# Half of an expert table and its sub-keys laid out by feature ahead of the launch, and a quarter of a dot fewer per block

## The chip, the cores and the metric

The kernel runs on one core of a Trainium2 chip. A core has TensorE (PE in the profile; its weight loads are PEld), VectorE (DVE), ScalarE (ACT), GpSimd (POOL) and SyncE (SP); sixteen DMA engines move data between the memory outside (HBM) and the core's SBUF. TensorE writes its results to PSUM, eight banks of 128 x 512 float32. SP issues plain loads and stores, POOL the indirect loads that gather rows by a list of indices. Each engine runs its own instructions in their order and waits on semaphores for the others.

The metric is the device time of one execution in microseconds (us), the median of several runs. The work that the host does to lay arrays out ahead of the launch is not in it.

## The reference, cut to what matters

One layer of a decoder over 256 prompt tokens and 8 x 4 sample tokens: a projection, two groups of heads (RWKV-7 and sparse attention), an output projection with a layer norm, and then the part that the change touches, a mixture of 16384 experts, each one row of two tables `u_tab` and `v_tab` (16384 x 2048, float32):

```python
def peer_ffn(x, wq, subkeys, u_tab, v_tab):
    q = (xt @ wq).reshape(n, P_HEADS, 2, P_DKEY // 2)
    s = jnp.einsum('nhcd,hckd->nhck', q, subkeys).astype(jnp.float32)
    hv, hix = lax.top_k(s, P_TOPK)
    ...
    tv, tpos = lax.top_k(cand, P_TOPK)
    expert = jnp.take_along_axis(cand_e, tpos, axis=-1)
    gate = jax.nn.softmax(tv, axis=-1).astype(x.dtype)
    ...
        h = jax.nn.gelu(jnp.einsum('cd,chkd->chk', xb, u_tab[eb]), approximate=False)
        return jnp.einsum('chk,chkd->cd', gb * h, v_tab[eb])
```

Eight heads choose 16 experts for each token, by scores against 2 x 8 sets of 128 sub-keys. For each choice the token's vector is multiplied with a row of `u_tab`.

## The kernel before

The kernel is one function, `hybrid_decode_step`, in stages; `kernel` around it hands the arrays over and starts it. Its pools of tiles lie on the left and the right of SBUF, and a tile that takes the place of an older one waits until that is free. The order of the instructions on each engine is made when the program is built: a scheduler simulates a timeline and takes what it holds to be ready, unless `high_priority`, `issue_after` or `keep_in_program_order` say otherwise. A load that moves to another place in that simulated time thus shifts its neighbours too.

The stages that matter here:

- **Sample rows** (`sample_chain`, up to some 1124 us). The 32 sample tokens run through output projection, queries, scores and their own dots, with weights loaded into a ring of ten buffers (`cw`). `subkeys` (L1424) loads the sub-keys as 128 rows of 128, turns them with 16 transposes on TensorE and copies them from PSUM into SKT on ScalarE (L1432). The last step is a Gelu on ScalarE (L1560) behind the last dot.
- **`wq`** (to some 1240 us). A second SKT is made in the same way for the prompt tokens. Then 16 chunks of `peer_wq` are multiplied with the tokens laid out by feature, XT, in float32 (L1813), the result is copied into QP (L1814), scored against SKT (L1370), and VectorE finds the top 16.
- **`peer`**, the dense loop, `for i1 in range(P): dense(i1)`. The product of the tokens with `u_tab` is split by features. The second half, features 1024 to 2047, is computed densely: for all 16384 experts, in 128 blocks of 128. A block's table rows are loaded by SP into `ur` (L1844, 128 x 1024, three buffers, NUR), turned by eight transposes on TensorE into PSUM `pt` (L1849), and split into two float32r parts: `uh`, rounded by ScalarE (L1644), and `ul`, the remainder, by VectorE (L1645). The tokens have been split in the same way into XHd and XLd. Three products of the parts, for eight blocks of 128 features, make 24 matmuls (L1855) into `ph`, which ScalarE copies to AW (L1857).
- **Dots.** The first half, features 0 to 1023, is done only for the chosen experts: POOL gathers 128 table rows of 1024 (L449, tile `rows`, five buffers, NRW), one for each token of a tile, and VectorE multiplies them with the tokens and sums along the row (L1779). There are 256 of these dots. Five or six are done in `wq`; the loop does ND = 1 per block and one more in NDN of 8 blocks; the rest, `left`, is spread over the first 28 steps of the next stage.
- **`weigh`**. 64 steps pick each choice's value out of AW: VectorE makes one-hot rows (L1887, `oo`), TensorE multiplies (L1899, L1929), VectorE sums (L1910, `xj`). The order here is held as written.
- **V**. The second table's half of the work, a dense product with `v_tab`. The change does not touch it.

Of the kernel before, what the change touches and what calls it, by code (L numbers as in the profile page):

```python
# [11 lines left out]
F32R = mybir.dt.float32r  # L12
# [6 lines left out]
P = 128  # L19
# [3 lines left out]
NPR = 256  # L23
# [12 lines left out]
WB = 4  # L36
# [10 lines left out]
NDW = 1  # L47
NPRI = 12
ND = 1
NDN = 4  # L50
NUR = 3
NRW = 5
WF = 3
PRO = 400
PRR = 0
# [90 lines left out]
def hybrid_decode_step(ctx: ExitStack, tc: tile.TileContext, a, outs, dbg=None):  # L146
    nc = tc.nc
    ve, sc, pe, gp, sy = nc.vector, nc.scalar, nc.tensor, nc.gpsimd, nc.sync
    stop = dbg.get("stop", 99) if dbg is not None else 99
# [99 lines left out]
    ident = C0("ident")  # L249
# [1131 lines left out]
    def choose(t, h, pool, S, TV):  # L1381
# [39 lines left out]
        ve.reciprocal(sm8, sm8)  # L1421
        ve.tensor_tensor(ge, ge, sm8[:, :, None].to_broadcast([P, n, 16]), OP.mult)

    def subkeys(raw, dst, tag):  # L1424

        for hf in range(2):
            sy.dma_start(raw[hf], a["peer_subkeys"][0].rearrange("h c k d -> k (h c) d")[:, 8 * hf:8 * hf + 8])
        for q in range(4):
            pb = bank(tag)
            for e in range(4):  # L1430
                pe.transpose(pb[:, 128 * e:128 * e + 128], raw[q // 2][:, 4 * (q % 2) + e, :], ident)
            sc.copy(dst[:, 4 * q:4 * q + 4, :].rearrange("p a b -> p (a b)"), pb)  # L1432

    def gate_rows(t_, u_):

        sy.dma_start(t_, a["rwkv_g2"][0, 0:128, :])
# [26 lines left out]
    utab, vtab = a["peer_u"][0], a["peer_v"][0]  # L1463
# [6 lines left out]
    def sample_chain(cx):  # L1470
        ring = lambda: cx([P, 1024], "cw", bufs=NCW)
        g2a, g2b = ring(), ring()
        gate_rows(g2a, g2b)
        pb = bank("ss")
# [56 lines left out]
        turned(X1s, x1s)  # L1531
        yield 1
        SKT, QPs, TV = cx([P, 16, P], "SKT"), cx([P, 16, 32], "QPs"), cx([P, 2, 16], "TV2")
        subkeys([ring().rearrange("p (k d) -> p k d", k=8) for _ in range(2)], SKT, "ss")
        yield 1
        qs = cx([P, 512], "qs", tag="xr_")

# [85 lines left out]
    def x1c(t, c0, n):  # L1623

        return X1[t][c0 // 1024][:, c0 % 1024:c0 % 1024 + n]
# [16 lines left out]
    def columns(pb, xh, xl):  # L1642

        sc.copy(xh, pb)  # L1644
        return ve.tensor_tensor(xl, pb, xh.bitcast(F32), OP.subtract)  # L1645
# [67 lines left out]
    bp_.close()  # L1713
    xq = Pool("xq", "right")
    XT = xq([P, 16, NPR], "XT")
    XH, XL = (xq([P, 8, NPR], nm, F32R) for nm in ("XHq", "XLq"))

    M_("ln1")
    gb1 = {}
# [4 lines left out]
    for t in range(2):  # L1724
        layer_norm(lp, lambda c0, n: x1c(t, c0, n),
                   *(lambda c0, n, nm=nm: gb1[nm, c0 // 1024][:, c0 % 1024:c0 % 1024 + n] for nm in ("ln1_g", "ln1_b")))
        for hf in range(2):
            sy.dma_start(X1D[P * t:P * t + P, 1024 * hf:1024 * hf + 1024], X1[t][hf])
        for q in range(4):
            pb = bank("pa")  # L1730
            for e in range(4):
                pe.transpose(pb[:, 128 * e:128 * e + 128], x1c(t, 512 * q + 128 * e, 128), ident)
            tk = slice(P * t, P * t + P)
            k4, p4 = slice(4 * (q % 2), 4 * (q % 2) + 4), pb.rearrange("p (k t) -> p k t", k=4)
            sc.copy(XT[:, 4 * q:4 * q + 4, tk], p4)
            if q > 1:
                columns(p4, XH[:, k4, tk], XL[:, k4, tk])
    oe.close()
    lp.close()
    cx[0].close()  # L1740
# [14 lines left out]
    HD = [up([P, P], f"hd{t}") for t in range(2)]  # L1755
    TV = [up([P, 8, 16], f"TV{t}") for t in range(2)]
    kc, dp, kq = (Pool(nm, "left") for nm in ("kc", "dp", "kq"))
    XHd, XLd = dp([P, 8, NPR], "XHd", F32R), dp([P, 8, NPR], "XLd", F32R)
    SKT = kq([P, 16, P], "SKT")
    QP = kq([P, 16, NPR], "QP")  # L1760

# [37 lines left out]


    kw_ = Pool("kw", "right")
    subkeys([kw_([P, 8, P], "wraw", bufs=WB) for _ in range(2)], SKT, "pb")
    hits = []
    for h in range(9):
        S = []
        for c in (2 * h, 2 * h + 1):
            if c < 16:
                pb = bank("pj")
                for o in range(0, 16, 8):
                    w = kw_([P, 8, P], "wraw", bufs=WB)  # L1810
# [18 lines left out]
    kw_.close()  # L1829
    sc.copy(XHd, XH)  # L1830
    sc.copy(XLd, XL)
    xq.close()
    kq.close()
    M_("peer")
    banks(pt=3, ph=2, pb=3)
    for t in range(2):
        gates(t, up, TV[t])
    aw = Pool("aw", "right")
# [1 line left out]

    def dense(i1):

        w = dp([P, 1024], "ur", bufs=NUR)
        sy.dma_start(w, utab[P * i1:P * i1 + P, 1024:])  # L1844
        ph = bank("ph")
        for q in range(2):
            pb = bank("pt")
            for e in range(4):
                pe.transpose(pb[:, 128 * e:128 * e + 128], w[:, 512 * q + 128 * e:512 * q + 128 * e + 128], ident)  # L1849
            wh, wl = dp([P, 4, P], "uh", F32R, bufs=2), dp([P, 4, P], "ul", F32R, bufs=2)  # L1850
            with tc.high_priority(offset=120 + 45 * i1 if i1 < NPRI else 0):
                lo_ = columns(pb.rearrange("p (k t) -> p k t", k=4), wh, wl)
            for e in range(4):
                for wi, xi in ((wh, XHd), (wh, XLd), (wl, XHd)):
                    mm = pe.matmul(ph[:, :NPR], wi[:, e, :], xi[:, 4 * q + e, :NPR],  # L1855
                                   start=(q == 0 and e == 0 and wi is wh and xi is XHd), stop=(q == 1 and e == 3 and wi is wl))
        return lo_, mm, sc.copy(AW[:, i1 // 64, :, i1 % 64], ph[:, :NPR])  # L1857

    tabled = []
    for i1 in range(P):  # L1860
        lo_, mm, end = dense(i1)
        n_ = ND + (i1 * NDN % 8 < NDN)
        with tc.issue_after(lo_.ins):
# [86 lines left out]
    raw = {}  # L1950
# [29 lines left out]
    pb = bank("pb")  # L1980
# [50 lines left out]
    for k in range(P):  # L2031
# [90 lines left out]
```

## Time and profile before

| | us |
|---|---|
| three runs | 2581.37, 2557.7, 2567.01 |
| median | 2567.01 |
| the profiled execution, its own time | 2586.08 |
| its span, first to last instruction | 2583.8 |
| mean granted TensorE clock | 0.93 |

The page begins with the busy time of each engine over the whole span:

```profile
PE 2310.9 (89%) x17452; PEld 1961.9 (76%) x17452; DVE 1939.6 (75%) x4264; ACT 1014.9 (39%) x1852; POOL 1328.2 (51%) x1393
```

Then it cuts the span into 40 slices of 64.6 us; each digit is the busy share in tenths, PEclk the granted clock:

```profile
PE   7989999988889987389799999996699799989996
DVE  4789756553654549859987888889976689888988
PEclk9999999987888978689899999996899899999998
DMA  7877974456579848975599999996678689898894
```

The dense loop is the run of slices with 9 in PE and DMA at once (some 1240 to 1740 us, slices 20 to 27). Two of the costliest groups of the page, by line (operation, output from inputs, shapes, count; busy us and mean ns of one; idle time of the engine just before them, and what ended it):

```profile
L449 POOL DMA_INDIRECT rows<-in_peer_u,gi x256 | 302.6, 1182 | 308.5 <-DVE rows L1779 273.9
L1849 PE MATMUL pt<-CT,ur 128*128 128x128 f32 x1024 | 149.4, 274 | 0.0
```

The mean of one matmul is its latency; since matmuls are pipelined, the time between two starts is shorter and is read from the chain or the timeline. A dot is an instruction L1779 with a short one that reads its sum; here too the next begins before the last one's recorded end.

### The profile page before, as it was taken

The numbers are of one execution on the slowest core, as the hardware profiler recorded it, in microseconds if no ns is written. First come the engines' busy times: TensorE is split into PE (matmuls) and PEld (weight loads), VectorE is DVE, ScalarE is ACT, GpSimd is POOL, SyncE is SP. The second block draws the span as 40 slices with busy tenths as digits, with TensorE's granted clock in tenths as the row PEclk, the third lists the DMA queues.
The fourth block names the chain that finished last, engine by engine and source line by source line (L and its number), as shares of the span: only waits on it lengthen the run. The fifth ranks groups of instructions, "written<-read, shape, count | busy, mean of one in ns | idle before, by whom it ended". The sixth has DMA issues, their size and how long they took to land.

```text
span 2583.8 us, 47156 instructions
## 1 busy us (share of the span) xinstructions
PE 2310.9 (89%) x17452; PEld 1961.9 (76%) x17452; DVE 1939.6 (75%) x4264; ACT 1014.9 (39%) x1852; POOL 1328.2 (51%) x1393
## 2 busy tenths in 40 slices
PE   7989999988889987389799999996699799989996
PEld 7878898866455655268799999996576688878885
DVE  4789756553654549859987888889976689888988
ACT  3433222223433432211244444444466444444443
POOL 6677424232543107636544444445555577767772
PEclk9999999987888978689899999996899899999998
DMA  7877974456579848975599999996678689898894
GB/s 222 235 224 232 273 215 143 130 182 227 214 216 315 263 158 301 313 240 163 207 371 342 349 353 346 348 333 223 219 252 279 236 324 325 325 340 322 324 323 171
DMA packets 347110, 683.46 MB, mean 265 GB/s; under 512 B 82174, under 2 KB 204992, under 8 KB 345824
## 3 DMA queue, kind: packets, MB, share of 16 engines
q1 hardware_dynamic: 249856, 343.76, 41.1%
q0 software_dynamic: 97024, 336.68, 36.7%
q8 instruction: 138, 2.26, 0.4%
q14 instruction: 92, 0.75, 0.1%
HBM read 664.77 MB, written 23.88 MB: 267 GB/s over the span
## 4 chain that ended last, share of the span: by engine, by line
PE 65%; DVE 13%; DMA 9%; issue 5%; POOL 4%; ACT 2%; SPq 1%; DVEq 0%; another core or an unknown queue 0%; POOLq 0%; ACTq 0%
PE pb L2047 19%; PE ph L1855 13%; PE pj L418 7%; PE pt L1849 4%; PE p L1075 2%; PE pa L1673 2%; DMA co<-in_cache_cmp_kv,gidx 2%; DVE rows L1779 2%; PE pa L1929 1%; PE pj L1813 1%; DVE cw L1557 1%; PE px L1899 1%; PE fs L1947 1%; PE sa L916 1%; DMA co<-in_cache_sel_kv,sidx 1%
## 5 line engine op out<-in xcount | busy, mean ns | idle before, releaser
L449 POOL DMA_INDIRECT rq<-in_peer_v,gi x256 | 377.4, 1474 | 168.1 <-DVE fP L2021 76.9
L449 POOL DMA_INDIRECT rows<-in_peer_u,gi x256 | 302.6, 1182 | 308.5 <-DVE rows L1779 273.9
L1855 PE MATMUL ph<-XHd,ul 128*128 128x256 f32 x1024 | 305.0, 298 | 17.2 <-DVE ul L1645 15.8
L1779 DVE SCALAR_TENSOR_TENSOR rows<-rows,x1a 128x1024 f32<-128x1024 f32 x256 | 309.0, 1231 | 4.4 <-DMA rows<-in_peer_u,gi 4.4
L1855 PE MATMUL ph<-XHd,uh 128*128 128x256 f32 x1024 | 297.1, 290 | 0.3 <-ACT uh L1644 0.3
L1855 PE MATMUL ph<-XLd,uh 128*128 128x256 f32 x1024 | 290.5, 284 | 0.0
L1644 ACT CAST uh<-pt 128x512 fp32r<-128x512 f32 x256 | 149.8, 587 | 277.0 <-PE ph L1855 193.4
L418 PE MATMUL pj<-XH,wl 128*128 128x288 f32 (+1 forms) x752 | 232.3, 309 | 12.5 <-DVE wl L413 7.2
L418 PE MATMUL pj<-XH,wh 128*128 128x288 f32 (+1 forms) x752 | 230.3, 306 | 14.0 <-DVE ss L748 7.0
L1645 DVE TENSOR_TENSOR ul<-pt,uh 128x512 fp32r<-128x512 f32 x256 | 175.9, 689 | 81.7 <-ACT uh L1644 73.8
L418 PE MATMUL pj<-XL,wh 128*128 128x288 f32 (+1 forms) x752 | 226.4, 301 | 0.0
L2047 PE MATMUL pb<-vl,ah 128*128 128x512 f32 x768 | 217.7, 392 | 0.0
L2047 PE MATMUL pb<-vh,al 128*128 128x512 f32 x768 | 216.5, 390 | 0.0
L2047 PE MATMUL pb<-vh,ah 128*128 128x512 f32 x768 | 199.1, 395 | 17.4 <-ACT vh L2040 17.4
L1855 PEld LDWEIGHTS ph<-XHd,ul 128*128 128x128 f32 x1024 | 196.9, 192 | 19.4 <-DVE ul L1645 17.7
L411 ACT CAST wh<-wraw 128x512 fp32r<-128x512 f32 (+1 forms) x188 | 114.6, 616 | 228.8 <-PE pj L418 170.2
L1855 PEld LDWEIGHTS ph<-XHd,uh 128*128 128x128 f32 x1024 | 197.3, 193 | 0.9 <-ACT uh L1644 0.5
L1855 PEld LDWEIGHTS ph<-XLd,uh 128*128 128x128 f32 x1024 | 196.8, 192 | 0.0
L2021 DVE SCALAR_TENSOR_TENSOR fP<-rq,ge,fP 128x512 f32<-128x512 f32 x254 | 189.7, 747 | 2.4
L2047 PEld LDWEIGHTS pb<-vh,ah 128*128 128x128 f32 x768 | 146.2, 191 | 48.8 <-ACT vh L2040 18.4
L2047 PEld LDWEIGHTS pb<-vl,ah 128*128 128x128 f32 x768 | 145.9, 190 | 30.6
L2047 PEld LDWEIGHTS pb<-vh,al 128*128 128x128 f32 x768 | 144.9, 189 | 30.4
(861 smaller groups left out, 5502.1 us busy)
## 6 DMA issues: line engine op xcount, KB each, us to landing
ur<-in_peer_u SPq DMA_DIRECT2D x128, 512.0 KB
wraw<-in_w_in SPq DMA_DIRECT2D x152, 256.0 KB
cw<-in_w_out SPq DMA_DIRECT2D x32, 512.0 KB
wraw<-in_w_out SPq DMA_DIRECT2D x32, 512.0 KB
cw<-in_peer_wq SPq DMA_DIRECT2D x32, 512.0 KB
wraw<-in_peer_wq SPq DMA_DIRECT2D x32, 512.0 KB
wraw<-in_w_in SPq DMA_DIRECT2D x64, 128.0 KB
co<-in_state_win_kv SPq DMA_DIRECT2D x16, 512.0 KB
```

What stands on the lines that cost most here:

```text
L411: sc.copy(wh[:, :, :n], w[:, :, :n])
L418: last[2] = pe.matmul(pb[:n, :nt], wi[:, k, :n], xi[(o + k) // 8][:, (o + k) % 8, :nt], start=(o + k == 0 and wi is wh and xi is xh), stop ...
L449: gp.indirect_dma_start(out=dst, out_offset=None, in_=rows_, in_offset=bass.IndirectOffsetOnAxis(ap=ix, axis=0))
L1075: pe.matmul(pb[hs[c], 64 * m:64 * m + 64], lhs(hs[c], m), rhs(hs[c], m), start=True, stop=True)
L1644: sc.copy(xh, pb)
L1645: return ve.tensor_tensor(xl, pb, xh.bitcast(F32), OP.subtract)
L1673: pe.matmul(acc[t], xi[:, e, P * t:P * t + P], wi[:, e, :], start=(k == e == n_ == 0), stop=(k == 6 and e == 1 and n_ == 2))
L1779: i_ = ve.scalar_tensor_tensor(r_, r_, 1.0, X1a[t], op0=OP.mult, op1=OP.mult, accum_out=h_)
L1849: pe.transpose(pb[:, 128 * e:128 * e + 128], w[:, 512 * q + 128 * e:512 * q + 128 * e + 128], ident)
L1855: mm = pe.matmul(ph[:, :NPR], wi[:, e, :], xi[:, 4 * q + e, :NPR], start=(q == 0 and e == 0 and wi is wh and xi is XHd), stop=(q == 1 and ...
L2021: ve.scalar_tensor_tensor(fP[t], r_, w_, fP[t], op0=OP.mult, op1=OP.add)
L2047: pe.matmul(acc[3 * t + q], wi[:, P * t:P * t + P], xi[:, 512 * q:512 * q + 512], start=(k == 0 and wi is ah and xi is vh), stop=(k == P - ...
```

## The change

Three things change at once.

1. **The layout of arrays.** `kernel` hands over `peer_u_t`, the second half of the first table with, for each block of 128 experts, the features in the rows: row p of a block holds, for eight blocks of features, feature p of the 128 experts. The sub-keys come as `subkeys_t`, with their inner dimension in the rows. The transposes on TensorE, the copies of SKT and the function `subkeys` are gone, and the PSUM banks of `pt` go to `ph` (five instead of two). `ur` is now read directly by ScalarE, VectorE and TensorE. `peer_subkeys` is no longer an input of the program; `peer_u` stays for the gathers.
2. **NSP = 6 of 8.** Only six of the eight blocks of features are split into float32r parts (18 matmuls, `uh` and `ul` of 128 x 384, three buffers each); the other two are multiplied in float32 as they are, with Xfd, a copy out of XT, and come first in each block (L1841 after the change).
3. **NDN = 2 instead of 4**, so every fourth block does a second dot, not every second.

```diff
-NDN = 4
+NDN = 2
+NSP = 6
...
-        subkeys([ring().rearrange("p (k d) -> p k d", k=8) for _ in range(2)], SKT, "ss")
+        sy.dma_start(SKT, a["subkeys_t"])
...
-    XH, XL = (xq([P, 8, NPR], nm, F32R) for nm in ("XHq", "XLq"))
+    XH, XL = (xq([P, NSP, NPR], nm, F32R) for nm in ("XHq", "XLq"))
...
-    subkeys([kw_([P, 8, P], "wraw", bufs=WB) for _ in range(2)], SKT, "pb")
+    sy.dma_start(SKT, a["subkeys_t"])
...
+    sc.copy(Xfd, XT[:, 8 + NSP:, :])
...
-    banks(pt=3, ph=2, pb=3)
+    banks(ph=5, pb=3)
...
-        w = dp([P, 1024], "ur", bufs=NUR)
-        sy.dma_start(w, utab[P * i1:P * i1 + P, 1024:])
+        w = dp([P, 8, P], "ur", bufs=NUR)
+        sy.dma_start(w.rearrange("p k e -> p (k e)"), a["peer_u_t"][P * i1:P * i1 + P, :])
         ph = bank("ph")
+        for e in range(NSP, 8):
+            pe.matmul(ph[:, :NPR], w[:, e, :], Xfd[:, e - NSP, :], start=(e == NSP), stop=False)
         for q in range(2):
-            pb = bank("pt")
-            for e in range(4):
-                pe.transpose(pb[:, 128 * e:128 * e + 128], w[:, 512 * q + 128 * e:512 * q + 128 * e + 128], ident)
-            wh, wl = dp([P, 4, P], "uh", F32R, bufs=2), dp([P, 4, P], "ul", F32R, bufs=2)
+            wh, wl = (dp([P, NSP // 2, P], nm, F32R, bufs=3) for nm in ("uh", "ul"))
             with tc.high_priority(offset=120 + 45 * i1 if i1 < NPRI else 0):
-                lo_ = columns(pb.rearrange("p (k t) -> p k t", k=4), wh, wl)
-            for e in range(4):
+                lo_ = columns(w[:, NSP // 2 * q:NSP // 2 * q + NSP // 2, :], wh, wl)
+            for e in range(NSP // 2):
                 for wi, xi in ((wh, XHd), (wh, XLd), (wl, XHd)):
-                    mm = pe.matmul(ph[:, :NPR], wi[:, e, :], xi[:, 4 * q + e, :NPR],
-                                   start=(q == 0 and e == 0 and wi is wh and xi is XHd), stop=(q == 1 and e == 3 and wi is wl))
+                    mm = pe.matmul(ph[:, :NPR], wi[:, e, :], xi[:, NSP // 2 * q + e, :],
+                                   start=False, stop=(q == 1 and e == NSP // 2 - 1 and wi is wl))
...
+    arrays["in_peer_u_t"] = np.ascontiguousarray(
+        u_[:, 1024:].reshape(P, P, 8, P).transpose(0, 3, 2, 1)).reshape(P * P, 1024)
+    arrays["in_subkeys_t"] = np.ascontiguousarray(k_.reshape(16, P, P).transpose(2, 0, 1))
```

How the order of the instructions moves is shown at three places. The first is TensorE in the middle of the dense loop. Before, four transposes stand between the matmuls of each half block:

```order
L1855 MATMUL ph<-XHd,uh 128x256
L1855 MATMUL ph<-XLd,uh 128x256
L1849 MATMUL pt<-CT_61,ur 128x128 x4
L1855 MATMUL ph<-XHd,ul 128x256
L1855 MATMUL ph<-XHd,uh 128x256
```

After, the two float32 matmuls of a block, with `ur` as it was loaded, stand between the last product of one block and the first of the next:

```order
L1848 MATMUL ph<-XLd,uh 128x256
L1848 MATMUL ph<-XHd,ul 128x256
L1841 MATMUL ph<-Xfd,ur 128x256 x2
L1848 MATMUL ph<-XHd,uh 128x256
L1848 MATMUL ph<-XLd,uh 128x256
```

A block has 24 rows of L1855 and eight of L1849 before, 18 of L1848 and two of L1841 after; no row of TensorE writes `pt` from `ur` any more.

The second place is VectorE in two steps of `weigh`: dots (`rows,hd`) between the one-hot rows `oo` and the sums `xj`. Before:

```order
L1779 SCALAR_TENSOR_TENSOR rows,hd_12236<-rows,x1a_12232 128x1024 x2
L1887 TENSOR_TENSOR oo<-CT_61,TB 128x1024
L1918 TENSOR_TENSOR TB<-E,TB 128x8
L1910 SCALAR_TENSOR_TENSOR xj,E<-px,oo 128x128 x4
L1779 SCALAR_TENSOR_TENSOR rows,hd_12236<-rows,x1a_12232 128x1024 x2
```

After:

```order
L1772 SCALAR_TENSOR_TENSOR rows,hd_12209<-rows,x1a_12205 128x1024 x3
L1880 TENSOR_TENSOR oo<-CT_61,TB 128x1024
L1911 TENSOR_TENSOR TB<-E,TB 128x8
L1903 SCALAR_TENSOR_TENSOR xj,E<-px,oo 128x128 x4
L1772 SCALAR_TENSOR_TENSOR rows,hd_12209<-rows,x1a_12205 128x1024 x3
```

Three or four dots stand in each of the 28 steps instead of two or three: 90 instead of 58 in all, and 161 instead of 193 in the loop.

The third place is the sub-keys. On ScalarE, before, the four copies SKT stand between the Gelu `hd` that ends the sample rows and the first copies QP of `wq`:

```order
L1560 ACTIVATE hd<-hd 128x32
L1432 COPY SKT<-pb 128x512 x4
L1814 COPY QP<-pj 128x256 x2
L1830 COPY XHd<-XHq 128x2048
L1831 COPY XLd<-XLq 128x2048
```

After, QP stands directly behind the Gelu:

```order
L1551 ACTIVATE hd<-hd 128x32
L1807 COPY QP<-pj 128x256 x2
L1823 COPY XHd<-XHq 128x1536
L1824 COPY XLd<-XLq 128x1536
L1825 COPY Xfd<-XT 128x512
```

On SP, at the beginning of the output projection (some 762 us of the trace before), the queue read:

```order
L1437 DMA cw<-in_rwkv_g 32x1024
L1499 DMA cw<-in_w_out 128x1024 x3
L1650 DMA x_00_9703<-in_x_prompt 128x1024
L1650 DMA x_01_9704<-in_x_prompt 128x1024
L1650 DMA x_10_9705<-in_x_prompt 128x1024
```

and after the change:

```order
L1428 DMA cw<-in_rwkv_g 32x1024
L1490 DMA cw<-in_w_out 128x1024 x3
L1525 DMA SKT<-in_subkeys_t 128x2048
L1804 DMA wraw<-in_peer_wq 128x8x128 x4
L1641 DMA x_00_9703<-in_x_prompt 128x1024
```

The sample's sub-keys and the first four loads of `peer_wq` have moved there, the latter from behind the stores of the normed tokens (L1728), since the buffers that `subkeys` took are free.

More of the change, by code (lines that the diff above doesn't have):

```diff
@@ L1422, in gates @@
         ve.tensor_tensor(ge, ge, sm8[:, :, None].to_broadcast([P, n, 16]), OP.mult)
[L1424 to L1429, printed above, removed]
-            for e in range(4):
-                pe.transpose(pb[:, 128 * e:128 * e + 128], raw[q // 2][:, 4 * (q % 2) + e, :], ident)
-            sc.copy(dst[:, 4 * q:4 * q + 4, :].rearrange("p a b -> p (a b)"), pb)
     def gate_rows(t_, u_):
@@ L1733, in hybrid_decode_step @@
             tk = slice(P * t, P * t + P)
-            k4, p4 = slice(4 * (q % 2), 4 * (q % 2) + 4), pb.rearrange("p (k t) -> p k t", k=4)
+            n4 = min(4, NSP - 4 * (q % 2))
+            k4, p4 = slice(4 * (q % 2), 4 * (q % 2) + n4), pb.rearrange("p (k t) -> p k t", k=4)
             sc.copy(XT[:, 4 * q:4 * q + 4, tk], p4)
             if q > 1:
-                columns(p4, XH[:, k4, tk], XL[:, k4, tk])
+                columns(p4[:, :n4], XH[:, k4, tk], XL[:, k4, tk])
     oe.close()
@@ L1757, in hybrid_decode_step @@
     kc, dp, kq = (Pool(nm, "left") for nm in ("kc", "dp", "kq"))
-    XHd, XLd = dp([P, 8, NPR], "XHd", F32R), dp([P, 8, NPR], "XLd", F32R)
+    XHd, XLd = dp([P, NSP, NPR], "XHd", F32R), dp([P, NSP, NPR], "XLd", F32R)
+    Xfd = dp([P, 8 - NSP, NPR], "Xfd")
     SKT = kq([P, 16, P], "SKT")
@@ L1841, in dense @@
     def dense(i1):
-        w = dp([P, 1024], "ur", bufs=NUR)
-        sy.dma_start(w, utab[P * i1:P * i1 + P, 1024:])
+        w = dp([P, 8, P], "ur", bufs=NUR)
+        sy.dma_start(w.rearrange("p k e -> p (k e)"), a["peer_u_t"][P * i1:P * i1 + P, :])
         ph = bank("ph")
+        for e in range(NSP, 8):
+            pe.matmul(ph[:, :NPR], w[:, e, :], Xfd[:, e - NSP, :], start=(e == NSP), stop=False)
         for q in range(2):
-            pb = bank("pt")
-            for e in range(4):
-                pe.transpose(pb[:, 128 * e:128 * e + 128], w[:, 512 * q + 128 * e:512 * q + 128 * e + 128], ident)
-            wh, wl = dp([P, 4, P], "uh", F32R, bufs=2), dp([P, 4, P], "ul", F32R, bufs=2)
+            wh, wl = (dp([P, NSP // 2, P], nm, F32R, bufs=3) for nm in ("uh", "ul"))
             with tc.high_priority(offset=120 + 45 * i1 if i1 < NPRI else 0):
-                lo_ = columns(pb.rearrange("p (k t) -> p k t", k=4), wh, wl)
-            for e in range(4):
+                lo_ = columns(w[:, NSP // 2 * q:NSP // 2 * q + NSP // 2, :], wh, wl)
+            for e in range(NSP // 2):
                 for wi, xi in ((wh, XHd), (wh, XLd), (wl, XHd)):
-                    mm = pe.matmul(ph[:, :NPR], wi[:, e, :], xi[:, 4 * q + e, :NPR],
-                                   start=(q == 0 and e == 0 and wi is wh and xi is XHd), stop=(q == 1 and e == 3 and wi is wl))
+                    mm = pe.matmul(ph[:, :NPR], wi[:, e, :], xi[:, NSP // 2 * q + e, :],
+                                   start=False, stop=(q == 1 and e == NSP // 2 - 1 and wi is wl))
         return lo_, mm, sc.copy(AW[:, i1 // 64, :, i1 % 64], ph[:, :NPR])
@@ L2112 @@
     arrays = {f"in_{n}": np.ascontiguousarray(inputs[n]) for n in _INS}
+    u_, k_ = arrays["in_peer_u"][0], arrays.pop("in_peer_subkeys")[0]
+    arrays["in_peer_u_t"] = np.ascontiguousarray(
+        u_[:, 1024:].reshape(P, P, 8, P).transpose(0, 3, 2, 1)).reshape(P * P, 1024)
+    arrays["in_subkeys_t"] = np.ascontiguousarray(k_.reshape(16, P, P).transpose(2, 0, 1))
     for g in range(len(_CONST)):
```

## The prediction

> **What bounds the kernel now.** I read the page first (chain of waits), then the windows, then the chain and the timeline in order of time. The page gives the spans and the shares of the chain:
>
> ```profile
> span 2583.8 us, 47156 instructions
> PE 65%; DVE 13%; DMA 9%; issue 5%; POOL 4%; ACT 2%; SPq 1%; DVEq 0%; another core or an unknown queue 0%; POOLq 0%; ACTq 0%
> ```
>
> TensorE ends 65% of the span, but an average hides the stages. The windows (busy us of PE, PEld, DVE, ACT, POOL with their counts, then granted clock, DMA share, GB/s) part the stretch that the change touches:
>
> ```profile
> 1243.00:1290.00 47.00, 38.83 (x281) 37.57 (x282) 41.42 (x121) 15.79 (x28) 24.02 (x32) 0.88 0.69 245
> 1280.00:1350.00 70.00, 68.03 (x579) 67.62 (x578) 60.57 (x100) 30.68 (x54) 30.65 (x32) 1.00 0.99 375
> 1290.00:1738.00 448.00, 446.91 (x3803) 445.59 (x3802) 366.78 (x606) 202.29 (x357) 208.52 (x181) 1.00 0.96 350
> 1738.00:1877.00 139.00, 90.23 (x534) 82.79 (x533) 132.94 (x390) 62.04 (x164) 76.42 (x58) 0.77 0.68 225
> ```
>
> The third row is the dense loop in its steady state: TensorE is never idle (446.91 of 448), so TensorE bounds it, while the DMA engines are at 0.96 of their time: a second bound stands right behind the first. The fourth row is the first part of `weigh`, where VectorE is busy 132.94 of 139 us and TensorE waits. So work taken from TensorE in the loop counts until DMA binds, and a dot moved from the loop into `weigh` counts in full.
>
> **The dense loop, price by price.** The chain shows the matmuls of one block beginning one period after the last:
>
> ```profile
> 1304.18 2.88 PE ph L1855 x24
> 1307.93 2.87 PE ph L1855 x24
> 1151.61 13.81 PE pj L1813 x64
> ```
>
> A block takes 1307.93 - 1304.18 = 3.75 us: 24 matmuls in float32r in 2.88 (0.120 each) and, in the other 0.87, the eight transposes. The window of 448 us holds 448 / 3.75 = 119 blocks; nine lie ahead of it. The third line prices what is added: `wq` multiplies float32 tiles of the same 128x128 by 128x256, each as two records, and 64 records take 13.81 us, 0.216 each. Two float32 matmuls per block are four records, 0.86 us. So on TensorE a block becomes 18 x 0.120 + 0.86 = 3.02 us, 0.73 less.
>
> VectorE, from its timeline:
>
> ```profile
> 1502.94 0.69 DVE L1645 TENSOR_TENSOR ul<-pt,uh 128x512 fp32r<-128x512 f32 x1 [0.16 <-ACT uh L1644]
> 1503.54 1.22 DVE L1779 SCALAR_TENSOR_TENSOR rows<-rows,x1a 128x1024 f32<-128x1024 f32 x1
> 1799.84 1.22 DVE L1779 SCALAR_TENSOR_TENSOR rows<-rows,x1a 128x1024 f32<-128x1024 f32 x1
> 1800.98 1.22 DVE L1779 SCALAR_TENSOR_TENSOR rows<-rows,x1a 128x1024 f32<-128x1024 f32 x1
> 1802.13 1.22 DVE L1887 TENSOR_TENSOR oo<-CT,TB 128x1024 f32<-128x1024 f32 x1
> ```
>
> From start to start, a dot takes 1.145 us and the 128x512 subtraction 0.60. Of 128x384, both inputs now from SBUF, it has no row: between 0.45 (by columns) and 0.60. Taking 0.45, a block asks 1.25 x 1.145 + 2 x 0.45 = 2.33 us of VectorE, with 0.60 it is 2.63; neither reaches 3.02. ScalarE rounds less than now (202.29 of 448 us busy). Both are hidden by TensorE or DMA.
>
> DMA: a load of `ur` and a gather of `rows` are 0.524 MB each. Now 1 + 1.5 of them pass per block, 1.311 MB in 3.75 us, which is the 350 GB/s of the row. After, 1 + 1.25 pass: 1.180 MB. At 3.02 us that would be 391 GB/s, and here the reading must choose. The highest rate that the loop shows over many blocks is the window 1280 to 1350: 375 GB/s at a share of 0.99, where VectorE was catching up with dots. That is nearest to a loop that asks for all it can get, so I take it: 1.180 MB / 375 GB/s = 3.15 us per block, 0.60 less than now, and the loop passes from TensorE to DMA. 119 x 0.60 = 72 us. The ends are 3.02 us (TensorE, 87 us gained) and 350 GB/s kept, 3.37 us (45 gained).
>
> DMA: Bandwidth & Descriptors, of the Trainium skill (Specifications), puts the share of one core in the HBM at about 358 GB/s; by that alone the block would be 3.30 us and the gain 54 instead of 72. The same pages, in HBM Reference (Specifications), say that a core that streams alone measures about 425; the 375 above speaks for the second.
>
> What else could hold the loop is the order of waits. The load of a later block now waits for VectorE's subtraction, no longer for the transposes (queue of SP, 1400 to 1700 us):
>
> ```profile
> SPq L1844 <- PE pt L1849: 263.9, 79, 3.7
> POOL rows L449 <- DVE rows L1779: 141.5, 77, 3.2
> ```
>
> SP and POOL both stand idle until a buffer comes free (3.3 us on average in SP's row), so buffers, not issue, pace them. VectorE runs its rows in order: a gather that is late holds the dot, behind it the next subtraction, then TensorE. The two float32 matmuls need only the load, so TensorE has 0.86 us that do not hang on that.
>
> The nine blocks ahead of 1290 took 47 us, more than 5 each, under waits for VectorE's top-16 search and for first gathers; I count no gain there (0 to 9 x 0.73 = 6.6).
>
> **The dots that move.** Every second block did two dots, now every fourth: 32 fewer in the loop, so 90 instead of 58 in the first 28 steps of `weigh`. VectorE binds there: 32 x 1.145 = 37 us back. POOL's gathers go with them:
>
> ```profile
> 1801.34 1.68 POOL L449 DMA_INDIRECT rows<-in_peer_u,gi  x1 [1.92 <-DVE rows L1779]
> 1803.32 0.94 POOL L449 DMA_INDIRECT rows<-in_peer_u,gi  x1 [0.30 <-issue]
> 1806.05 1.68 POOL L449 DMA_INDIRECT rows<-in_peer_u,gi  x1 [1.80 <-DVE rows L1779]
> ```
>
> A step of two dots is 4.71 us; three or four dots make it about 6.0. POOL issues three gathers in some 4.2 us and waits for VectorE today, so it keeps up. If gathers paced the step instead, a dot would cost 4.71 / 2 = 2.36 us and the 32 would cost 75; VectorE's 96% says 37.
>
> **The sub-keys.** Ahead of `wq`, ScalarE sits in order behind the Gelu of the sample rows:
>
> ```profile
> 1124.33 0.23 ACT hd L1560
> 1124.93 1.56 ACT SKT L1432 x3
> 1126.49 0.28 ACT QP L1814
> 1126.82 9.19 PE pj L1813 x32
> 1105.19 8.95 DMA cw<-in_peer_u,gi
> 1115.74 7.00 DMA cw<-in_peer_u,ig
> ```
>
> TensorE has filled its two banks and waits for the copy QP, which stands behind four copies SKT. Without them it resumes some 2.0 us sooner. The 1 MB of SKT now lands directly; it is first read at the scores, 9.19 us later, behind a chunk of `wq` that covers it. The transposes of the sample's own SKT lie beside a stream of weight loads: zero.
>
> The free slots let SP issue this sample SKT and four loads of `in_peer_wq`, 3 MB, at about 763 us, ahead of four `x` loads and `in_w_out`. At 375 GB/s that is up to 8 us of delay for products queued behind them. In return 1 MB leaves the stretch at 843 us, and 2 MB leave the time near 1090 to 1124, where dots wait for gathers (last two lines). I take zero for the pair, with 6 us either way. The casts and copies of `XH`, `XHd` in ScalarE get shorter by a quarter or less and lie beside the loads of `wq`: zero.
>
> **The sum.** -72 (loop) + 37 (dots) - 2 (QP) = -37 us. The profiled execution took 2586.08 us with what lies around its span, 19 above the median of the runs, 2567.01; against its own time the sum is 2549, and against the median 2530, 1.4% less. I state the latter, since the median is what is compared. About 1% (26 us, to 2541) is what a measurement can tell from no change: the runs before spread from 2557.7 to 2581.37.
>
> **The rivals.**
>
> *TensorE stays the bound.* If DMA moves 391 GB/s when asked, the block is 3.02 us: -87 + 37 - 2 = -52, 2515. For it: share 0.99 at 375 GB/s would give 379 when full, and loads laid end to end may do better than half rows. Against it: no 70 us of the loop show 391. Chance 0.22.
>
> *DMA is nearly full already.* 350 GB/s at 0.96 would be 365 at full share, 3.23 us, and at 350 kept it is 3.37. The gain is 45 to 62, the sum -10 to -27, 2540 to 2557. For it: four hundred us at 0.96. Against it: the 375. Chance 0.24.
>
> *Slower.* Late gathers hold VectorE, TensorE idles, and its clock falls as between 1243 and 1290:
>
> ```profile
> PEld ph L1855 <- DVE ul L1645: 16.0, 5, 8.5
> ```
>
> There waits of up to 8.5 us went with a clock of 0.88. At 0.88 the 3.02 become 3.43, and with 5% idle 3.61: 119 x 0.14 = 17 gained, 37 - 2 lost, +18, 2585. It turns into a loss from 3.46 us per block. For it: five row buffers and three of `ur`, all in order behind VectorE. Against it: with 2 us idle in 70 the clock stayed 1.00. Chance 0.10, of which 0.06 beyond 1%.
>
> TensorE: Matmul & The Clock Gate, of the Trainium skill (Part 1), has the clock halve after about 3.4 us without work; waits of 0.1 to 0.3 us per block would not reach that, as the row with 2 us idle in 70 agrees.
>
> **How the numbers follow.** The forecast (3.05 to 3.23 us per block) has 0.44, and its own range is 2515 to 2541. Faster by over 1% are all of it but 0.02 and the first rival: 0.64. Within 1% lie the second rival, 0.02 of the forecast and 0.04 of the third: 0.30. Slower: 0.06. The range starts from 2515 less 6.6 (early blocks) and 6 (loads), 2502, and goes to 2557 plus 6 and some 9 for gathers that pace `weigh` in part, 2572.
>
> **What would show it.** Right: loop windows at 365 to 385 GB/s with DMA share 0.98 or more, TensorE busy 95%, clock 1.00, some 3.15 us between blocks; `weigh` up to its last dot 176 us long instead of 139; QP directly after the Gelu. Wrong: TensorE at 100% and 3.02 us (first rival), 350 GB/s (second), VectorE waiting for gathers and a clock below 0.95 (third), or a `weigh` over 185 us.

## The result

| | runs | median us | lowest to highest | ratio to before, 95% interval |
|---|---|---|---|---|
| before | 16 | 2569.20 | 2555.01 to 2581.99 | |
| after | 16 | 2545.15 | 2525.09 to 2566.59 | 0.9907 [0.9886, 0.9928] |

The change takes 0.93% off the time, 24 us. The forecast was 2530, 37 us less; the time lies inside the range, and just short of the 1% that the prediction took as the least that can be told from no change. The ratio leaves out one run after, 2566.59 us, which was over 1.5% above the fastest.

The profiled execution after took 2551.85 us. Its page gives span and shares of the chain:

```profile
span 2549.9 us, 44379 instructions
PE 59%; DVE 15%; DMA 12%; issue 6%; POOL 5%; ACT 1%; SPq 1%; DVEq 0%; POOLq 0%; ACTq 0%
```

TensorE ends 59% of the span instead of 65%, DMA 12% instead of 9%. The windows of the kernel after (busy us of PE, PEld, DVE, ACT, POOL with counts; granted clock, DMA share, GB/s) are the first blocks, the rest of the loop, a steady stretch in it, and `weigh` up to the last dot:

```profile
1223.00:1267.00 44.00, 36.95 (x234) 33.70 (x235) 42.23 (x149) 16.34 (x34) 27.89 (x41) 0.92 0.55 190
1267.00:1662.00 395.00, 378.77 (x2593) 344.73 (x2591) 298.37 (x553) 178.97 (x354) 220.18 (x157) 1.00 0.97 365
1400.00:1600.00 200.00, 196.01 (x1345) 178.37 (x1346) 149.82 (x282) 93.81 (x185) 110.46 (x76) 1.00 0.97 363
1662.00:1839.00 177.00, 104.23 (x531) 96.28 (x531) 169.40 (x454) 62.48 (x166) 124.59 (x89) 0.68 0.80 266
```

In the third row TensorE works 196.01 of 200 us, and the DMA engines are busy for 0.97 of their time. By busy shares alone either could be the bound. The fourth row is `weigh` as forecast: 177 us, VectorE busy 169.40 of them.

The two timelines, cut at the same events (the first load of `rwkv_g`, the Gelu of the samples, the last matmul of `wq`, the ends of copies 10, 30 and 128 of `ph` to AW, the last dot, the end), say where the time went:

| stretch | before us | after us | difference | forecast |
|---|---|---|---|---|
| start to the first load of `rwkv_g` | 761.6 | 744.0 | -17.6 | 0 |
| to the Gelu | 362.7 | 372.4 | +9.7 | 0 ± 6 |
| to the end of `wq` | 107.7 | 106.0 | -1.7 | -2 |
| to block 10 | 63.2 | 44.7 | -18.5 | 0 (to -6.6) |
| to block 30 | 74.6 | 73.3 | -1.3 | -12 (20 x 0.60) |
| to block 128 | 369.6 | 321.3 | -48.3 | -59 (98 x 0.60) |
| to the last dot | 137.6 | 177.1 | +39.5 | +37 |
| to the end | 706.8 | 711.1 | +4.3 | 0 |

The first row is no part of the change. All 13 kernels profiled here issue the same instructions up to that load, and it came between 744.0 and 763.6 us. It flatters this pair of executions: without it the rows give -16, with it -34; the medians say -24. The 4.3 us behind the last dot are left open: there the three kernels with the old dense half took 706.1 to 706.8 us, and the ten with the new one 706.7 to 712.3.

Blocks 30 to 128 took 321.3 / 98 = 3.28 us each, not 3.15. The chain of the kernel after, through one cycle of four blocks, shows why (start, length in us, what; L1841 are the float32 matmuls, L1848 those in float32r):

```profile
1462.10 2.17 PE ph L1848 x18
1464.27 0.02 issue
...
1464.68 0.53 ACT uh L1635
...
1465.24 0.57 DVE ul L1636
...
1465.85 2.18 PE ph L1848 x16
1468.03 0.86 PE ph L1841 x4
1468.89 2.36 PE ph L1848 x18
1471.26 0.87 PE ph L1841 x4
...
1477.31 0.02 issue
```

Ordinary blocks last 0.87 + 2.15 = 3.02 us, the forecast's price on TensorE. But from 1464.27 to 1465.85 the chain leaves TensorE: copy AW, cast `uh`, subtraction `ul`, matmuls again. The cycle repeats after 1477.31 - 1464.27 = 13.04 us, 3.26 per block. The timelines of ScalarE and VectorE there (idle time ahead and its releaser in brackets):

```profile
1461.27 0.61 ACT L1850 COPY AW<-ph 128x256 f32<-128x256 f32 x1 [0.69 <-PE ph L1848]
1464.29 0.59 ACT L1850 COPY AW<-ph 128x256 f32<-128x256 f32 x1 [2.40 <-PE ph L1848]
1464.68 0.93 ACT L1635 CAST uh<-ur 128x384 fp32r<-128x384 f32 x2
1465.24 1.03 DVE L1636 TENSOR_TENSOR ul<-ur,uh 128x384 fp32r<-128x384 f32 x2 [2.92 <-ACT uh L1635]
```

Two copies AW follow each other with no cast between. The second must wait for its block's matmuls, so ScalarE idles 2.40 us and VectorE 2.92, and the casts of the *next* block, queued behind that copy, come only when TensorE has run dry. Its two float32 matmuls cover 0.86 us of this, and the rest is idle. In ScalarE's rows as the program has them, this happens at every fourth copy (60, 64, 68, ...), once per two-dot block.

So there are two theories for the loop. **A**: DMA is the bound, at 363 GB/s instead of my 375, so that a block moves its 1.180 MB in 3.26 us. **B**: TensorE stays the bound, with one gap in four blocks from ScalarE's order. For the stretch up to the Gelu, theory **H** says that the loads moved ahead delay what is queued behind them; its rival says that +9.7 us is chance, a difference between two executions.

### The profile page after: what moved, and what is told of

Read it like the earlier page. It is cut to its first block, busy times and chain, and to the rows that moved or that the text cites. A ratio compares the mean times of both kernels' runs of the same rounds, so it can differ in the third digit from the quotient of the medians.

```text
span 2549.9 us, 44379 instructions
## 1 busy us (share of the span) xinstructions
PE 2250.9 (88%) x16140; PEld 1870.8 (73%) x16140; DVE 1901.8 (75%) x4264; ACT 985.3 (39%) x1845; POOL 1380.0 (54%) x1393
## 3 DMA queue, kind: packets, MB, share of 16 engines
q1 hardware_dynamic: 245984, 343.76, 40.8%
## 4 chain that ended last, share of the span: by engine, by line
PE 59%; DVE 15%; DMA 12%; issue 6%; POOL 5%; ACT 1%; SPq 1%; DVEq 0%; POOLq 0%; ACTq 0%
PE pb L2040 20%; PE ph L1848 9%; PE pj L419 7%; DVE rows L1772 3%; DMA rows<-in_peer_u,gi 3%; PE ph L1841 2%; PE pa L1664 2%; PE pj L1806 2%; DMA co<-in_cache_cmp_kv,gidx 2%; PE p L1076 2%; DVE CA L473 1%; PE pa L1922 1%; PE ss L1492 1%; DMA big<-in_state_rwkv 1%; PE px L1892 1%
## 5 line engine op out<-in xcount | busy, mean ns | idle before, releaser
L450 POOL DMA_INDIRECT rows<-in_peer_u,gi x256 | 356.0, 1391 | 231.1 <-DVE rows L1772 181.0
L1848 PE MATMUL ph<-XHd,uh 128*128 128x256 f32 x768 | 239.1, 311 | 4.1 <-ACT uh L1635 0.8
L1848 PE MATMUL ph<-XHd,ul 128*128 128x256 f32 x768 | 225.2, 294 | 15.4 <-DVE ul L1636 13.1
L1848 PE MATMUL ph<-XLd,uh 128*128 128x256 f32 x768 | 218.1, 284 | 0.0
L1636 DVE TENSOR_TENSOR ul<-ur,uh 128x384 fp32r<-128x384 f32 x256 | 135.2, 559 | 88.0 <-ACT uh L1635 87.1
L2040 PEld LDWEIGHTS pb<-vh,ah 128*128 128x128 f32 x768 | 146.3, 191 | 48.9 <-ACT vh L2033 18.5
L473 DVE SCALAR_TENSOR_TENSOR CA<-co,wbc,CA 128x256 f32<-128x256 f32 x248 | 135.9, 585 | 51.6 <-DMA co<-in_cache_cmp_kv,gidx 51.5
L1635 ACT CAST uh<-ur 128x384 fp32r<-128x384 f32 x256 | 125.5, 515 | 111.9 <-PE ph L1848 54.3
L1848 PEld LDWEIGHTS ph<-XHd,ul 128*128 128x128 f32 x768 | 147.6, 193 | 27.1 <-DVE ul L1636 26.3
L419 PEld LDWEIGHTS pj<-XH,wl 128*128 128x128 f32 (+1 forms) x752 | 143.7, 191 | 27.4 <-DVE wl L414 10.9
```

Source lines behind the costliest of these rows:

```text
L419: last[2] = pe.matmul(pb[:n, :nt], wi[:, k, :n], xi[(o + k) // 8][:, (o + k) % 8, :nt], start=(o + k == 0 and wi is wh and xi is xh), stop ...
L450: gp.indirect_dma_start(out=dst, out_offset=None, in_=rows_, in_offset=bass.IndirectOffsetOnAxis(ap=ix, axis=0))
L473: ve.scalar_tensor_tensor(d_, x_, w_, d_, op0=OP.mult, op1=OP.add)
L1848: mm = pe.matmul(ph[:, :NPR], wi[:, e, :], xi[:, NSP // 2 * q + e, :], start=False, stop=(q == 1 and e == NSP // 2 - 1 and wi is wl))
```

## The experiments

### The loop: is it DMA?

*No float32 matmuls* (the kernel after, as in all experiments unless said otherwise):

```diff
-        for e in range(NSP, 8):
-            pe.matmul(ph[:, :NPR], w[:, e, :], Xfd[:, e - NSP, :], start=(e == NSP), stop=False)
```

> The two float32 matmuls of each dense block are left out, and with them two of the eight blocks of features of the first table's dense half; all loads and gathers stay. Theory A (DMA is the bound of the changed loop, 1.180 MB per block at some 363 GB/s): the block stays at 3.2 to 3.3 us although TensorE has 0.86 us less to do, and TensorE's busy share falls below 80%. Theory B (TensorE's 3.02 us, and one wait per four blocks in the order of ScalarE and VectorE behind the three load buffers, make the 3.26): the block falls to 2.4 to 2.9 us and the DMA rate rises to 400 GB/s or more.

The kernel leaves out two of the eight blocks of features, so its output is not the layer's. It took 2524.93 us in one run (span 2523.0). Blocks 30 to 128 took 3.08 us each. In its loop (window columns as above):

```profile
1450.00:1630.00 180.00, 147.76 (x1076) 134.01 (x1076) 144.98 (x274) 88.51 (x179) 110.07 (x76) 0.99 1.01 392
```

With the same bytes per block the transfers now take 392 GB/s at a full share. So 363 was not their limit, and theory A in its plain form falls. But the block did not come to B's 2.4 to 2.9 us either, nor to the 2.16 us of 18 matmuls: at 392 GB/s its bytes ask 1.180 MB / 392 = 3.01, and every fourth block still lasted 3.78. This run does not part these two.

*Four load buffers* (and, to make room, two instead of three of `uh` and `ul`):

```diff
-NUR = 3
+NUR = 4
...
-            wh, wl = (dp([P, NSP // 2, P], nm, F32R, bufs=3) for nm in ("uh", "ul"))
+            wh, wl = (dp([P, NSP // 2, P], nm, F32R, bufs=2) for nm in ("uh", "ul"))
```

> Four load buffers for the table instead of three, paid for with two buffers each for the split parts instead of three. Theory A: DMA has no more to give, the block stays at 3.2 to 3.3 us. Theory B: the wait for a free buffer goes, and the block comes to 3.02 to 3.10 us, 119 blocks x 0.2 = 24 us less than the changed kernel.

2558.31 us (2546.49 to 2567.19), ratio 0.9932 [0.9908, 0.9957]. Later blocks take 3.02, 3.02, 2.72 and 4.08 us in turn, 3.21 on average: the gap stays, at another place of the cycle, and two copies AW still stand in a row once in four blocks. Four more dots are left for `weigh`, which takes 185 us up to its last dot. The stretch to block 10 is 53.5 us instead of 44.7. A fourth load buffer does not remove the gap, and two buffers of `uh` and `ul` seem to cost some nine at the start. B had expected 3.02 to 3.10 here and A 3.2 to 3.3, so this run by itself speaks for A.

*All eight blocks split, no float32* (again with two buffers of `uh` and `ul`):

```diff
-NSP = 6
+NSP = 8
```

> All eight blocks of features are split into float32r parts and none is multiplied in float32 (two buffers for the parts, as before the change): TensorE has 24 x 0.120 = 2.88 us per block instead of 3.02, VectorE and ScalarE a third more of the split. Theory A: 3.2 to 3.3 us per block as in the changed kernel, same time. Theory B: 0.1 us less per block, some 12 us less; if VectorE (2 x 0.6 + 1.43 = 2.63 us) gets in the way in order, it could be as much more.

2567.11 us, ratio 0.9965 [0.9937, 0.9992]; blocks of 2.88, 3.09, 2.88 and 4.23 us, 3.27 on average. TensorE asks 2.88 us and is busy for only 92% of the time:

```profile
1400.00:1600.00 200.00, 184.78 (x1467) 177.98 (x1468) 167.57 (x280) 107.12 (x182) 90.95 (x78) 1.00 0.97 361
```

This row alone would again look like a limit of 361 GB/s, and A had expected this time. But a limit of the transfers would not by itself explain one long block in every four. It is not B's order either: casts and copies alternate on ScalarE here. TensorE waits mainly for the subtraction `ul` (15.0 us in these 200, in 17 waits), and in the two-dot block that stands behind two dots in a row on VectorE. That this order makes the long block was read from the trace and not tested.

*The copy held behind the next casts.* From block 12 on, `dense` does not issue its copy to AW at once; it is issued in the next block, behind both casts:

```diff
+            if q and held:
+                with tc.issue_after(last_[0].ins):
+                    held.append(sc.copy(*held.pop()))
...
-        return lo_, mm, sc.copy(AW[:, i1 // 64, :, i1 % 64], ph[:, :NPR])
+        end = held.pop() if held else None
+        out_ = (AW[:, i1 // 64, :, i1 % 64], ph[:, :NPR])
+        if NPRI <= i1 < P - 1:
+            held.append(out_)
+        else:
+            end = sc.copy(*out_)
+        return lo_, mm, end
```

Here `last_[0]` is the cast `uh` just issued. Nothing else changes: same loads, same dots, same matmuls.

> The changed kernel; from block 12 on the copy of a finished block (AW from ph) is queued on ScalarE behind both casts uh of the next block. In the changed kernel ScalarE's queue holds, once in four blocks, this copy with no cast of the next block ahead of it, and the trace shows a gap of about 0.75 us on TensorE there (three blocks of 3.02 us and one of 3.78, the next 3.22: 13.04 us for four). Theory B (order of ScalarE, TensorE otherwise the bound): all blocks near 3.02 to 3.08 us, 0.20 to 0.24 us less over 116 blocks, 23 to 28 us less than the changed kernel: ratio to before about 0.980 to 0.982. Theory A (the transfers are the bound at 363 GB/s): the gap moves to a wait for ur, the block stays at 3.26 us, ratio 0.990.

2522.26 us (2516.76 to 2539.11), ratio 0.9831 [0.9784, 0.9878], its interval clear of the 0.9907 [0.9886, 0.9928] of the kernel after. Chain and ScalarE's timeline:

```profile
1457.12 2.15 PE ph L1853 x18
1459.28 0.86 PE ph L1843 x4
1460.14 2.15 PE ph L1853 x18
1462.30 0.86 PE ph L1843 x4
```

```profile
1458.01 0.93 ACT L1637 CAST uh<-ur 128x384 fp32r<-128x384 f32 x2 [1.10 <-DMA ur<-in_peer_u_t]
1459.32 0.61 ACT L1850 COPY AW<-ph 128x256 f32<-128x256 f32 x1 [0.38 <-PE ph L1853]
1460.94 0.93 ACT L1637 CAST uh<-ur 128x384 fp32r<-128x384 f32 x2 [1.02 <-DMA ur<-in_peer_u_t]
1462.34 0.62 ACT L1850 COPY AW<-ph 128x256 f32<-128x256 f32 x1 [0.47 <-PE ph L1853]
```

Casts and copies alternate, and the chain stays on TensorE with 3.02 us per block. The windows:

```profile
1280.00:1350.00 70.00, 63.51 (x448) 59.80 (x449) 60.05 (x109) 32.98 (x64) 40.52 (x34) 1.00 1.03 408
1430.00:1630.00 200.00, 199.37 (x1448) 191.32 (x1448) 162.17 (x301) 100.82 (x198) 106.44 (x83) 1.00 1.01 388
```

The same loop moves 388 GB/s over 200 us, 408 over 70, with TensorE at 199.37 of 200. Theory B is shown and A is out: an order on an engine that is busy 47% of the time held the loop. By the ratios it cost 0.0076 x 2569 = 20 us; in the two profiles blocks 10 to 128 went from 394.6 to 368.9 us, 26 less. Theory B had 23 to 28. The three other kernels below with the copy held and 1.25 dots took 378.3 to 380.2 us there, so the 26 is the upper end. Blocks 30 to 128 took 300.4 to 305.5 us in the four, 3.07 to 3.12 each: most blocks last 3.02 us, but single longer ones are left, which no run explains.

### The loads that moved ahead

*Both held back to their old places:*

```diff
-        sy.dma_start(SKT, a["subkeys_t"])
+        with tc.issue_after(last[0].ins):
+            sy.dma_start(SKT, a["subkeys_t"])
...
-                    sy.dma_start(w, w_q[:, 128 * c:128 * c + 128].rearrange("(k p) c -> p k c", p=P)[:, o:o + 8])
+                    with tc.issue_after(last[1].ins):
+                        sy.dma_start(w, w_q[:, 128 * c:128 * c + 128].rearrange("(k p) c -> p k c", p=P)[:, o:o + 8])
```

`last[0]` is the samples' last weight load, `last[1]` the last store of the prompts' normalised rows.

> The sample's sub-keys and the first four loads of the query weights are held back to where they stood before the change; all else is the changed kernel. Theory H (3 MB moved ahead of the loads of the output projection delay it): from the first load of rwkv_g to the Gelu of the sample rows it takes 362 us again, as before the change, instead of 372, and the kernel is 8 to 10 us faster than the changed one, some 2536. Rival (those 10 us were chance, as the 17 us ahead of that load must be): 372 again, and no difference in time.

2545.24 us (2521.9 to 2548.99), ratio 0.9871 [0.9829, 0.9913] against 0.9907 [0.9886, 0.9928]: 9 us, with intervals that overlap, so that the times alone do not show a gain. The way to the Gelu took 349.7 us, where 362 had been expected. The queue of SP shows the mechanism, in the kernel before and then in the kernel after (start, time in which the row's loads were issued):

```profile
761.59 0.54 SPq L1436 DMA_DIRECT2D cw<-in_rwkv_g  x1
...
766.74 0.55 SPq L1436 DMA_DIRECT2D wraw<-in_rwkv_g  x1
```

```profile
744.00 0.54 SPq L1427 DMA_DIRECT2D cw<-in_rwkv_g  x1
...
746.52 0.41 SPq L1525 DMA_DIRECT2D SKT<-in_subkeys_t  x1
747.04 12.01 SPq L1804 DMA_DIRECT2D wraw<-in_peer_wq  x4
762.33 0.38 SPq L1427 DMA_DIRECT2D wraw<-in_rwkv_g  x1
```

The prompts' load of `rwkv_g` was issued 5.2 us after the samples' before, and 18.3 us after it now: SP issues in order, and its row of four `wq` loads alone lasts 12.01 us. The chain of the kernel after then waits for just that load:

```profile
762.33 10.59 DMA wraw<-in_rwkv_g
```

*One held, one ahead.* With the copy AW held as well (so against the run e10 below), once the sub-keys alone are held and once `wq` alone; and the kernel before with the sub-keys alone changed (both places of the call, here the second):

```diff
-    subkeys([kw_([P, 8, P], "wraw", bufs=WB) for _ in range(2)], SKT, "pb")
+    sy.dma_start(SKT, a["subkeys_t"])
```

> The copy held, the load of the sub-keys of the samples back in its old place, the four loads of wq still ahead. Measure: time from the first load of rwkv_g to the first product of the prompts with w_out (40.4 us before, 57.9 after, 40.8 with both held). If the bytes ahead set it, 2 of 3 MB give some 52 us; if it is the loads of wq alone, 57; if the sub-keys alone, 41.

> The copy held, the four loads of wq back in their old place, the load of the sub-keys of the samples still ahead. Same measure: by bytes some 46 us (the kernel before with the sub-keys alone showed 45.2), 41 if the loads of wq alone set it, 57 if the sub-keys do.

> The kernel before with the sub-keys alone laid out by feature (loaded directly, no transposes and no copies of them), dense half and dots as before. Prediction: -2 us at the copy QP after the Gelu of the samples, hoisted load 0 within 6: ratio 0.997 to 1.002. If the hoisted loads cost what holding them back gained (9 us or more): ratio 1.002 to 1.005.

The last gave 2570.26 us, ratio 1.0016 [0.9985, 1.0046]: no difference that can be told. The other two ran once each, 2535.98 and 2519.80 us. All 13 kernels, by what is loaded ahead of its old place; times from the first load of `rwkv_g`, each in its own profile:

| ahead of the old place | prompts' load of `rwkv_g` us | first product with `w_out` us | Gelu us |
|---|---|---|---|
| nothing: kernel before, the same with fewer dots (below) | 5.2, 4.6 | 40.4, 42.1 | 362.7, 357.7 |
| nothing: both held, alone and in the two kernels at the end | 5.9, 6.0, 5.9 | 40.8, 40.7, 42.8 | 349.7, 346.9, 353.9 |
| sub-keys: kernel before | 6.2 | 45.2 | 354.1 |
| sub-keys: with the copy held, all eight blocks split | 7.1, 8.5 | 44.3, 45.7 | 352.5, 352.0 |
| `wq`: with the copy held | 15.5 | 47.4 | 361.9 |
| both: kernel after, no float32, four loads, copy held | 18.3, 18.2, 18.8, 19.1 | 57.9, 57.0, 59.1, 58.3 | 372.4, 365.1, 372.9, 365.6 |

In the kernel with all eight blocks split the `wq` loads kept their old place, 87 us behind the first load, so it belongs with those that have the sub-keys alone ahead.

It is neither bytes alone (52 and 46 expected) nor one load alone: each delays the first product, by 6.7 and 3.6 us, and the two together by more than their sum, 17.2. Most of the delay in SP's queue comes from the `wq` loads. At the Gelu the four kernels with both loads ahead took 365.1 to 372.9 us and the three with both held 346.9 to 353.9: the two groups do not overlap, and their means are 19 us apart. So theory H holds, and its rival is out. Against the two kernels with the old layout the loads ahead cost 9 us, the forecast's own measure. The other ten, by which the changed kernel with both held is ahead of the old ones at the Gelu, were not in the forecast. With the sub-keys alone in the new layout the old kernel took 354.1, so a part of them may come from there; no run shows it.

### The dots alone

*The kernel before with fewer dots in the loop:*

```diff
-NDN = 4
+NDN = 2
```

> The kernel before with 1.25 dots a block instead of 1.5 and nothing else changed: every instruction of the dense half stays. If TensorE bounds the old loop, the block stays at 3.75 us and 32 dots move to the stretch behind it, which becomes 37 to 40 us longer: ratio 1.014 to 1.016. If the two-dot blocks held the old loop by VectorE or by the gathers' share of the transfers, the block falls below 3.75 us (by up to 0.3 us at the same GB/s, 1.311 to 1.180 MB) and the sum is from 0 to +20 us: ratio 1.000 to 1.008.

2608.38 us (2599.35 to 2614.74), ratio 1.0151 [1.0095, 1.0207]. The loop and `weigh` up to the last dot:

```profile
1290.00:1723.00 433.00, 429.94 (x3653) 429.39 (x3652) 317.84 (x516) 194.57 (x343) 153.74 (x142) 1.00 0.90 309
1724.00:1902.00 178.00, 102.65 (x531) 94.66 (x531) 170.53 (x454) 62.92 (x168) 122.93 (x90) 0.69 0.81 264
```

The old loop keeps its 3.75 us while DMA falls to 309 GB/s, so TensorE bounded it by itself. The 32 dots make the second stretch 39.6 us longer (137.6 to 177.2 from the end of the last copy AW). By itself this part of the change is a loss of 1.5%. Whether it pays beside the other two parts was not run: the changed kernel with 1.5 dots a block is missing, and with both repairs the two counts of dots cannot be told apart (below).

### Both repairs together

*The copy held and the loads held:* the two diffs above in one kernel.

> The copy held behind the next casts together with the loads of the sub-keys and of wq held back to their old places. Theory B with the hoisted loads costing what the run with them held back showed (ratio 0.987 against 0.991): both gains add, 23 to 28 us plus about 9, ratio 0.976 to 0.979. Theory A: the held loads alone, ratio 0.987. If the held loads' gain was chance: 0.981.

2504.56 us (2498.27 to 2509.92), ratio 0.9745 [0.9705, 0.9786]: 63 us less than the 2567.78 of the kernel before beside it, faster than the change as well. Against the copy held alone (0.9831) the loads count 0.0086, 22 us. By the medians of the two it is 18, and the six runs of each do not overlap (2516.76 us and up, 2509.92 and down). Blocks 50 to 90 take 3.02 us each, and from 1400 to 1600 us TensorE hardly waits:

```profile
1400.00:1600.00 200.00, 198.66 (x1440) 190.32 (x1439) 162.18 (x301) 101.84 (x196) 105.74 (x81) 1.00 1.00 386
```

*The same with 1.5 dots a block:* NDN = 4 in that kernel.

> The kernel with the copy and the loads held back, with 1.5 dots a block again. Per block it moves 1.311 MB. The transfers took 408 GB/s in the busiest 70 us seen so far, 386 over 200 us: then a block cannot go below 3.21 to 3.40 us, the loop is 22 to 45 us longer than the 3.02 to 3.04 us of the kernel with 1.25 dots, and the stretch behind it 39.5 shorter: ratio to before 0.967 to 0.977. If TensorE stayed the bound at 3.02 us (434 GB/s), the ratio would be about 0.960. If the gathers come too late for VectorE, waits on TensorE and over 3.5 us, ratio above 0.98.

2506.89 us (2500.29 to 2512.9), ratio 0.9772 [0.9734, 0.981]; it cannot be told from the one before. Blocks 10 to 128 take 407 us instead of 378, `weigh` is 39 us shorter. Here DMA is the bound. The window and the waits of the loop (us in total, times, longest):

```profile
1400.00:1600.00 200.00, 184.10 (x1283) 173.44 (x1282) 166.28 (x304) 89.51 (x175) 109.34 (x92) 0.98 1.01 394
ACT uh L1638 <- DMA ur<-in_peer_u_t: 67.5, 47, 2.9
DVE rows L1775 <- DMA rows<-in_peer_u,gi: 23.8, 41, 1.9
```

TensorE idles 16 of 200 us, loads and gathers are both late, and at 394 GB/s 1.311 MB need 3.33 us. Of the forecast 22 to 45 us in the loop it cost 29.

## Why the prediction was right, and where it was not

**The direction and the range** held: 24 us less against 37, in the range, and the terms of opposite sign were the right ones. That it would be over 1% was given 0.64; it came out at 0.93%.

**The dots.** Forecast +37 at 1.145 us each, measured +39.5, and +39.6 with nothing else changed. The upper end, gathers that pace `weigh`, did not come.

**The wait for the copy QP.** Forecast -2, the stretch from the Gelu to the end of `wq` got 1.7 us shorter. The sub-keys as a whole gained nothing in the kernel before (1.0016).

**The loop.** The prices on TensorE were right: 3.02 us per block stands in the loop of every kernel with two float32 blocks. The step that failed is "the loop passes from TensorE to DMA" at 375 GB/s. That figure came from a stretch of the kernel before in which TensorE was at 97%: a rate that was asked for, not a limit. The loop takes 386 to 408 when it asks for more. So the first rival, TensorE as the bound at 3.02 us, was the right mechanism, though even with the copy held the mean block lasted 3.07 to 3.12; I had written against it that no 70 us of the loop show 391. It did not show in the time because of something that no part of the prediction had: an order on ScalarE that lets the casts of the next block stand behind the copy of the last. I had called ScalarE hidden by its busy time, 202 of 448 us. The order of its instructions could have been read from the rows of the changed program: two copies in a row, once per two-dot block.

DMA: Bandwidth & Descriptors, of the Trainium skill (Specifications), with about 358 GB/s for one core's share of the HBM, would have given 3.30 us and thus nearly the measured 3.28. The runs do not bear out that reason: the same transfers ran at 388 over 200 us as soon as the order was mended.

**The early blocks.** I counted nothing for the first nine and 12 us for the next twenty; it was 18.5 and 1.3. The sum, 20 instead of 12, is nearer than the parts. With neither transposes nor `pt` to wait for, the first blocks ran ahead of the dots: 10 dots were done by block 10 instead of 19. From block 10 to 30 the loop then made 33 dots instead of 32 in the same time, with the DMA engines full:

```profile
1280.00:1350.00 70.00, 62.66 (x420) 56.84 (x420) 56.49 (x103) 28.35 (x59) 40.98 (x32) 0.98 0.98 380
```

In the two kernels with two buffers of `uh` and `ul` the early stretch took 53.5 and 54.9 us, so the third buffer seems to be about half of that gain; neither run changes the buffers alone, so this was not shown.

**The loads moved ahead.** Forecast 0 within 6 us, from bytes by bandwidth (3 MB, 8 us) set against what they no longer take later. It was +9.7 between the two profiles and +9 between the means of the two groups of kernels; holding the loads back gained 9 us (not clear of noise) and 22 by the ratios. The delay of the first half was right, but the step missed that SP issues in order: the row of `wq` loads holds the queue for 12 us, and the prompts' load of `rwkv_g` stands behind it. Nothing came back near the Gelu to make up for it: against the kernels with both held, the first product was 17 us late and the Gelu 19.

Put together, the loop with its early blocks gave 68 of the 72 us forecast. That this is so near is luck: blocks 30 to 128 fell 11 us short (48 of 59), from a rate taken too low and a gap not seen, and the early blocks gave 8 us more than I had counted. The medians miss the forecast by 13 us; in the two profiles the rows behind the first miss it by 21, of which the loads' 9.7 are the largest part.

## What to carry to other kernels

An engine that is busy 47% can still set the pace: read the order of its rows around the instruction that the bottleneck waits for, and ask whether something early-ready stands behind something that must wait for the bottleneck itself. A transfer rate seen while another engine is the bound is a lower bound on what the DMA engines can do; take it as a limit only from a stretch in which the compute engines wait for data. A load that a free buffer lets the scheduler move ahead costs its time in the issuing queue as well as its bytes: look at what is queued behind it.

## What was not expected of the hardware

One core's transfers, plain loads and gathers mixed, ran at 386 to 394 GB/s over 200 us and 408 over 70, where the kernel before gave 350 as its steady state. A DMA share near 1 did not tell how much was left: in the windows of the loop above, 0.96 to 0.99 stood beside 350 to 380 GB/s and 1.00 to 1.03 beside 386 to 408.

Issuing a gather on POOL got dearer as well: 110.46 / 76 = 1.45 us each in the steady loop of the kernel after, against 71.21 / 66 = 1.08 in the kernel before with NDN = 2, which makes the same number of dots per block:

```profile
1400.00:1600.00 200.00, 197.16 (x1676) 196.93 (x1674) 145.26 (x237) 89.35 (x158) 71.21 (x66) 1.00 0.91 315
```

That the subtraction `ul` now reads SBUF where it read PSUM is not enough to explain it. It reads SBUF also with four load buffers and with all eight blocks split, and there a gather took 87.78 / 78 = 1.13 and 90.95 / 78 = 1.17 us. What goes with the long ones in the traces is a dot on VectorE: in the same 200 us of all 13 kernels, 385 of the 393 gathers that start while a dot runs there (1.145 us from its start) last 1.6 us or more, and none of the other 638 does. Of such starts the kernel after has 46 of 76, and the kernel before with NDN = 2 has 13 of 65. POOL had room for it; why a dot has this effect was not tried.
